# Low-order parts of k in one zero-padded tile per head, so that both score products contract over 128 partitions

## The chip, the cores and the metric

The kernel runs on one core of a Trainium2 chip. Its engines work side by side, each on its own queue in order: TensorE (PE in the profile; PEld are its weight loads), VectorE (DVE), ScalarE (ACT), GpSimd (POOL) and SyncE (SP), which issues most of the DMAs. The metric is the device time of one execution in microseconds, the median of the runs. Times of single instructions come from one profiled execution.

## The reference

A decoder trunk of two layers over 512 tokens of width 1024, in float32. Each layer is half a feed-forward step, a mixer, and half a feed-forward step; a norm stands before each and at the end. The mixer has 12 heads of dilated window attention (three groups of four, with rotary positions on q and k) and 4 heads of stick-breaking attention, 64 features a head:

```
s = einsum('bhrnqd,bhrnkd->bhrnqk', qb, kw) * (dh ** -0.5)      # dilated: banded, causal, softmax
z = einsum('bhqd,bhkd->bhqk', q_blk, k) * (dh ** -0.5)          # stick-breaking
w = where(past, exp(log_sigmoid(z) + after), 0.0)               # after: sum of log_sigmoid(-z) between s and t
y = gate_dil * (o_dil @ w_proj_dil) + gate_sb * (o_sb @ w_proj_sb)
x = x + y @ w_out
```

## The kernel before

Activations lie feature-major, 128 features by 512 tokens in a tile. A float32 product is made of float32r passes: each operand is split into a high part and a low part (value minus high), and high x high, high x low and low x high are added in PSUM. For the large projections that is `mm3` (L141, its three matmuls on L142, L143, L144), fed by the class `Weights`, which streams 128x128 weight blocks from memory and splits them four at a time on ACT (L76) and DVE (L77).

Attention scores have only 64 features a head, and the kernel uses the other 64 partitions for the split. `qk_pair` (L348) projects q and then k of two heads (e = 0, 1) into one PSUM bank, 24 matmuls each. For q it makes a tile per head whose own half of the partitions holds the high part (ACT, L372) and whose other half holds the low part (DVE, L373). For k it makes a tile per head with the high part in its own half (L376) and, by a DMA between partitions, a copy of it in the other half (L377). One tile `kl` for both heads takes the low parts, head 0 in the lower half and head 1 in the upper (L378). With rotary positions ("rope"), DVE multiplies by the cosine table (L357) and shuffles partitions into `qb` (L358), and POOL multiplies and adds (L359, L360).

`scores` (L382) then makes one block of scores from two matmuls into the same PSUM columns: q tile x k high tile over 128 partitions (L384: high x high plus low x high), and q high x k low over the 64 partitions of the head (L385, the slices `own`). The stationary operand is the 128 columns of q in both, loaded for each matmul.

`stick` (L410) runs two heads, each with four query blocks against 128, 256, 384 and 512 keys: scores, a mask as one more matmul (L419), Abs, Exp and Ln on ACT, a scan and two more passes on DVE (L426 to L429), Exp on ACT (L430); then transposes (L439), a split of the transposed weights (`split_t`), and their products with the values (L443). `dil_scores` (L465) makes the scores of three dilated groups for a pair of head slots, 128 or 256 keys at a time, each block masked and reduced on DVE (L481, L497); `dil_softmax` and `dil_values` follow (transposes L556, L558, L573; products with values L565, L583). `gather_o` (L397) collects an output in the tile `of`. `fill` puts gate projections between these.

The mixer's main order in the program is V projection, q and k of heads 0 and 1, stick, q and k of heads 2 and 3, stick, then for two slot pairs scores, softmax and values, then gates and the output projection. The order in which each engine gets its instructions is set before the run by a planner with modelled times (`schedule_with_timeline_sim=True`), so projections of later heads stand between the attention blocks of earlier ones. Tiles are taken from pools with a fixed number of buffers: 10 for q and k tiles (five of them a pair), 2 for `qb`, 1 for `of`. A buffer is given again when its last reader is done.

Of the kernel before, what the change touches and what calls it, by code (L numbers as in the profile page):

```python
# [9 lines left out]
F32 = mybir.dt.float32  # L10
F32R = mybir.dt.float32r
# [4 lines left out]
P = 128  # L16
D = 1024
T = 512
# [12 lines left out]
TAIL = 2  # L31
HELD = KD
HT = T // 2
# Output tiles whose gates are projected after q and k of (slot pair, group);
# group 3 stands for the end of the slot pair.
GATES = {(0, 0): (), (0, 1): (0, 1), (0, 2): (), (0, 3): (2,), (1, 0): (3,), (1, 1): (), (1, 2): (), (1, 3): (4, 5, 6)}

# Activations are feature-major: [feature, token]. Token columns are ordered
# c = 128 j + 32 r + m for the token t = 128 j + 4 m + r ("nat" order); the
# dilated groups use (r, j, m) order ("perm": one 128-token tile per residue r  # L40
# modulo 4). Float32 products run as three float32r passes: hi*hi, hi*lo, lo*hi
# with lo = v - float32r(v).


class Weights:
    """Streams 128x128 weight blocks in order of use, split into hi and lo."""

    AHEAD = 2

# [56 lines left out]
def trunk(ctx, tc, xin, win, gains, rope, masks, out, depth):  # L106
    nc = tc.nc

    def pool(stack, name, bufs=1, **kw):
        return stack.enter_context(tc.tile_pool(name=name, bufs=bufs, reuse_waits="tile", **kw))  # L110
# [6 lines left out]
    npool = pool(ctx, "npool")  # L117
# [11 lines left out]
    for k in range(KD):  # L129
        t = xpool.tile([P, T], F32, name=f"x{k}", tag=f"x{k}")  # L130
# [24 lines left out]
            return nc.scalar.preload_act_table_set(name)  # L155

    class Norm:
        """Gathers the squares of x tile by tile; r = rsqrt(mean + eps)."""

        def __init__(self, g, table=None):  # L160
            self.g = g * KD
# [92 lines left out]
                finale(st, hs, nxt)  # L254

    def finale(st, hs, nxt):
        """The last output tiles by halves of the tokens, each followed by its final norm."""
        op = pool(st, "fin", 4)
        blocks = [[weights.block() for _ in hs] for _ in range(TAIL)]
        for c0 in range(0, T, HT):  # L260
            c = slice(c0, c0 + HT)
            for i, row in enumerate(blocks):
                d = KD - TAIL + i
                ps = bank("o")
                for f, (w, h) in enumerate(zip(row, hs)):
                    mm3(ps[:, :HT], w, [t[:, c] for t in h], f == 0, f == NF - 1)
                nc.vector.scalar_tensor_tensor(xs[d][:, c], ps[:, :HT], 0.5, xs[d][:, c], ALU.mult, ALU.add)
                nxt.square(d, c)
            nxt.finish(c0 // P, (c0 + HT) // P)
            for k in range(0, KD, 2):  # L270
                o = op.tile([P, 2, HT], F32, name="o", tag="o")
                eng = nc.gpsimd if k == 2 else nc.vector
                for i in range(2):
                    eng.tensor_mul(o[:, i], xs[k + i][:, c], nxt.rb[:, :HT])
                nc.sync.dma_start(out[k:k + 2, :, c].rearrange("k p t -> p k t"), o)

    def mixer(norm, nxt):
        outer = ExitStack()
        mp = pool(outer, "mix")
        st = ExitStack()  # L280
        vp = pool(st, "mixv")
        qp = pool(st, "mixq", 10)
        wk = pool(st, "mixw", 2)
        pp = pool(st, "mixp", 8)
        tp = pool(st, "mixt", 2)
# [1 line left out]
        h = norm.h  # L287

        def work(name):
            return wk.tile([P, T], F32, name=name, tag=name, bufs=1 if name == "of" else 2)  # L290

        spill = []
        for k in range(KD):
            t = dram.tile([P, T], F32, name="spill", tag="spill")
# [5 lines left out]
        nc.scalar.dma_start(cr, rope[0])  # L300
        nc.scalar.dma_start(sr, rope[1])

        # V, token-major: [token, head, hi|lo, 64]
        pv = []
        for half in range(2):
            pv.append([bank(b) for b in ("mmtt", "ssoo")[half]])
            for k in range(KD):
                wh, wl = weights.quarter()
                for j in range(NT):
                    c = slice(j * P, (j + 1) * P)  # L310
                    ps = pv[half][j]
# [15 lines left out]
            if half == 0:  # L327
                v0, vs = [], []
                for j in range(NT):
                    sc = norm.rt[:, j:j + 1]  # L330
                    for lst, nm, off in ((v0, "v0", 0), (vs, "vs", 256)):
                        t = vp.tile([P, 4, 2, HD], F32R, name=f"{nm}_{j}", tag=f"{nm}_{j}")
# [13 lines left out]
            return nat_view(ap)  # L346

        def qk_pair(kind, view_q, view_k):  # L348
            """Projects q and k of two heads; returns per head (q stack, k hi, k lo)."""
            res = []  # L350
            for which in ("q", "k"):
                ps = bank("m")
                project(ps, h)
                a = work("qa")
                if kind == "rope":
                    b = work("qb")
                    nc.vector.tensor_mul(a, ps, cr)  # L357
                    nc.vector.stream_shuffle(b, ps, ROT)  # L358
                    nc.gpsimd.tensor_mul(b, b, sr)  # L359
                    nc.gpsimd.tensor_add(a, a, b)  # L360
                else:
                    nc.vector.scalar_tensor_tensor(a, ps, SC if which == "q" else 1.0, norm.rb,
                                                   ALU.mult, ALU.mult)
                if which == "k":
                    kl = qp.tile([P, T], F32R, name="kl", tag="q")
                for e in range(2):
                    own = slice(64 * e, 64 * e + 64)
                    oth = slice(64 - 64 * e, 128 - 64 * e)
                    src = nat_view(a[own])
                    hi = qp.tile([P, T], F32R, name=which + "h", tag="q")  # L370
                    if which == "q":
                        nc.scalar.copy(view_q(hi[own]), src)  # L372
                        nc.vector.tensor_sub(view_q(hi[oth]), src, view_q(hi[own]).bitcast(F32))  # L373
                        res.append([hi])
                    else:
                        nc.scalar.copy(view_k(hi[own]), src)  # L376
                        nc.sync.dma_start(hi[oth].bitcast(F32), hi[own].bitcast(F32))  # L377
                        nc.vector.tensor_sub(view_k(kl[own]), src, view_k(hi[own]).bitcast(F32))  # L378
                        res[e] += [hi, kl, own]
            return res  # L380

        def scores(ps, qkv, qc, kc, start, stop=True):  # L382
            q, kh, kl, own = qkv
            nc.tensor.matmul(ps, q[:, qc], kh[:, kc], start=start, stop=False, skip_group_check=True)  # L384
            nc.tensor.matmul(ps, q[own, qc], kl[own, kc], start=False, stop=stop, skip_group_check=True)  # L385

        def tile_c(i, n=1):
            return slice(i * P, (i + n) * P)
# [6 lines left out]
            return hi, lo  # L395

        def gather_o(po, of, e):  # L397
            """Adds the Vh and Vl halves into of's half e."""
            own = slice(64 * e, 64 * e + 64)
            nc.scalar.copy(of[own], po[64:128])  # L400
            nc.vector.tensor_add(of[own], po[0:64], of[own])
# [57 lines left out]
        gates = {}  # L459
# [3 lines left out]
                gates[d] = (gate(d, 0), gate(d, 1))  # L463

        def dil_scores(s, st_a, st_b, pn, pm):  # L465
            """Scores, mask and running maximum of slots 2s, 2s+1."""
            qk0 = qk_pair("rope", same, same)
            fill(s, 0)
            for e in range(2):
                for i in range(2):  # L470
                    ps = bank("s")
                    for u in range(2):
                        j = 2 * i + u
                        c0 = 256 * u + (0 if j else P)
                        c1 = 256 * u + 256
                        scores(ps[:, c0:c1], qk0[e], tile_c(j), slice(max(j - 1, 0) * P, (j + 1) * P), u == 0)
                    for u in range(2):
                        j = 2 * i + u
                        lo_c = 0 if j else P
                        t = pn[e][j]  # L480
                        nc.vector.tensor_tensor_reduce(  # L481
                            t[:, lo_c:256], ps[:, 256 * u + lo_c:256 * u + 256], mnat[:, lo_c:256],
                            1.0, NEG, ALU.add, ALU.max, st_a[:, 0, e, j:j + 1])
            qk1 = qk_pair("rope", nat_to_perm, nat_to_perm)
            fill(s, 1)
            qk2 = qk_pair("rope", nat_to_perm, nat_to_perm)
            fill(s, 2)
            for e in range(2):
                for i in range(2):
                    ps = bank("s")  # L490
                    for u in range(2):
                        r = 2 * i + u
                        scores(ps[:, 256 * u:256 * u + P], qk1[e], tile_c(r), tile_c(r), u == 0)
                        scores(ps[:, 256 * u + P:256 * u + 256], qk2[e], tile_c(r), tile_c(r), False)
                    for u in range(2):
                        r = 2 * i + u
                        nc.vector.tensor_tensor_reduce(  # L497
                            pm[e][r], ps[:, 256 * u:256 * u + 256], mperm,
                            1.0, NEG, ALU.add, ALU.max, st_b[:, 0, e, r:r + 1])
# [111 lines left out]
        st = ExitStack()  # L611
# [64 lines left out]
ROT = list(range(8, 16)) + list(range(0, 8)) + list(range(16, 32))  # L676


# [1 line left out]
def _tokens():  # L680
    import numpy as np
    c = np.arange(T)
# [35 lines left out]


def _pack_layer(a, l):  # L720
    """Weight blocks [n, 128, 128] of one layer in the order of use."""
    import numpy as np

    def ffn(g, u, dn):
# [78 lines left out]
```

## Time and profile before

| | |
|---|---|
| median of 3 runs | 2210.35 us (2209.13 to 2211.56) |
| profiled execution, first to last instruction | 2208.9 us |
| DVE busy | 1192.9 us (54%) |
| ACT busy | 893.0 us (40%) |
| POOL busy | 366.1 us (17%) |
| mean granted TensorE clock | 0.992 |

A line of the engine views names the line of the kernel, the engine, the output tile and its inputs, the shape and how often it stands; "64*128 64x256" is a product that contracts over 64 partitions, has 128 output rows and streams 256 columns. The mixers lie at about 380 to 700 us and 1475 to 1790 us of the span. The granted clock is the share of full speed at which TensorE was let run.

### The profile page before, as it was taken

How to read it: one execution, taken by the hardware profiler on the slowest of the kernel's cores; microseconds unless marked ns; L12 is line 12 of the kernel's file. 1: busy time of each engine (PE TensorE's matmuls, PEld its weight loads, DVE VectorE, ACT ScalarE, POOL GpSimd, SP SyncE). 2: the span in 40 equal slices, each digit the busy share in tenths (PEclk: the TensorE clock that was granted, in tenths of full speed). 3: DMA queues.
4: the chain of work that ended last, by engine and by line, in shares of the span. 5: the costliest groups of instructions: out<-in, count | busy, mean ns of one | idle time of the engine just before them, and what ended most of it. 6: DMA issues, size and time to landing. Idle time of an engine off the chain costs nothing.

```text
span 2208.9 us, 25967 instructions
## 1 busy us (share of the span) xinstructions
PE 2187.1 (99%) x9828; PEld 1787.4 (81%) x9828; DVE 1192.9 (54%) x1892; ACT 893.0 (40%) x1572; POOL 366.1 (17%) x384
## 2 busy tenths in 40 slices
PE   8999999999999999999999999999999999999998
PEld 7888888877887888888888888888778788888887
DVE  5445433688757545543345544337887575544433
ACT  5333333566454433333233333236654454333332
POOL 2222100021312122210022220000123112222100
PEclk9999999999999999999999999999999999999999
DMA  4233333222213232232222333333222143333322
GB/s 150 95 96 96 100 114 120 88 90 77 77 62 124 96 96 96 96 96 95 96 96 96 96 96 105 109 119 96 81 70 79 58 134 96 96 96 98 99 91 86
DMA packets 64622, 212.81 MB, mean 96 GB/s; under 512 B 7408, under 2 KB 9456, under 8 KB 64496
## 3 DMA queue, kind: packets, MB, share of 16 engines
q1 hardware_dynamic: 63920, 210.10, 29.6%
q8 instruction: 77, 1.26, 0.2%
q10 hardware_dynamic: 576, 1.05, 0.2%
q14 instruction: 49, 0.40, 0.1%
HBM read 200.63 MB, written 6.29 MB: 94 GB/s over the span
## 4 chain that ended last, share of the span: by engine, by line
PE 98%; DVE 1%; ACT 0%; DMA 0%; POOL 0%; issue 0%; SPq 0%; DVEq 0%; POOLq 0%; ACTq 0%
PE ps_o L144 13%; PE ps_o L143 13%; PE ps_o L142 13%; PE ps_m L142 11%; PE ps_m L143 11%; PE ps_m L144 11%; PE ps_t L142 5%; PE ps_t L143 5%; PE ps_t L144 5%; PE ps_s L385 2%; PE ps_s L384 1%; PE ps_o L583 1%; PE ps_o L443 0%; PE ps_t L314 0%; PE ps_m L314 0%; PE ps_m L313 0%
## 5 line engine op out<-in xcount | busy, mean ns | idle before, releaser
L77 DVE TENSOR_TENSOR wlo<-wraw,whi 128x512 fp32r<-128x512 f32 x736 | 595.8, 812 | 617.5 <-ACT whi L76 616.6
L76 ACT CAST whi<-wraw 128x512 fp32r<-128x512 f32 x736 | 456.0, 621 | 1004.7 <-PE ps_o L143 489.4
L142 PE MATMUL ps_m<-xh,whi 128*128 128x512 f32 x992 | 395.3, 399 | 8.9 <-ACT whi L76 5.8
L143 PE MATMUL ps_m<-xl,whi 128*128 128x512 f32 x992 | 394.4, 398 | 0.0
L144 PE MATMUL ps_m<-xh,wlo 128*128 128x512 f32 x992 | 394.2, 397 | 0.0
L142 PE MATMUL ps_o<-fh,whi 128*128 128x512 f32 (+1 forms) x748 | 285.6, 382 | 0.0
L143 PE MATMUL ps_o<-fl,whi 128*128 128x512 f32 (+1 forms) x748 | 285.5, 382 | 0.0
L144 PE MATMUL ps_o<-fh,wlo 128*128 128x512 f32 (+1 forms) x748 | 285.5, 382 | 0.0
L239 POOL TENSOR_TENSOR fg<-fg,fs 128x512 f32<-128x512 f32 x88 | 114.9, 1307 | 928.7 <-ACT fs L238 928.7
L142 PEld LDWEIGHTS ps_m<-xh,whi 128*128 128x128 f32 x992 | 189.6, 191 | 51.1 <-ACT whi L76 6.7
L143 PEld LDWEIGHTS ps_m<-xl,whi 128*128 128x128 f32 x992 | 189.6, 191 | 40.0 <-DVE xl L180 0.8
L144 PEld LDWEIGHTS ps_m<-xh,wlo 128*128 128x128 f32 x992 | 189.8, 191 | 39.5 <-DVE wlo L77 0.2
L142 PE MATMUL ps_t<-xh,whi 128*128 128x512 f32 x480 | 187.0, 390 | 0.0
L143 PE MATMUL ps_t<-xl,whi 128*128 128x512 f32 x480 | 186.8, 389 | 0.0
L144 PE MATMUL ps_t<-xh,wlo 128*128 128x512 f32 x480 | 186.8, 389 | 0.0
L143 PE MATMUL ps_o<-xl,whi 128*128 128x512 f32 x448 | 174.3, 389 | 0.0
L142 PE MATMUL ps_o<-xh,whi 128*128 128x512 f32 x448 | 174.3, 389 | 0.0
L144 PE MATMUL ps_o<-xh,wlo 128*128 128x512 f32 x448 | 174.3, 389 | 0.0
L143 PEld LDWEIGHTS ps_o<-fl,whi 128*128 128x128 f32 x748 | 140.5, 188 | 30.2
L144 PEld LDWEIGHTS ps_o<-fh,wlo 128*128 128x128 f32 x748 | 140.4, 188 | 30.1
L142 PEld LDWEIGHTS ps_o<-fh,whi 128*128 128x128 f32 x748 | 140.5, 188 | 30.0
L240 POOL TENSOR_TENSOR fg<-fg,rb 128x512 f32<-128x512 f32 x88 | 114.9, 1307 | 6.3
(204 smaller groups left out, 2702.3 us busy)
## 6 DMA issues: line engine op xcount, KB each, us to landing
wraw<-in_w_dram SPq DMA_DIRECT2D x367, 512.0 KB, 3.4
spill<-x SPq DMA_DIRECT2D x16, 256.0 KB, 2.1
kh<-kh SPq DMA_DIRECT2D x32, 128.0 KB, 2.8
x<-spill SPq DMA_DIRECT2D x16, 256.0 KB, 3.4
x<-in_x_dram SPq DMA_DIRECT2D x8, 256.0 KB, 5.8
out_dram<-o SPq DMA_DIRECT2D x8, 256.0 KB, 3.0
wraw<-in_w_dram SPq DMA_DIRECT2D x2, 256.0 KB, 4.2
cr<-in_rope_dram ACTq DMA_DIRECT2D x2, 256.0 KB, 2.6
```

The costliest lines, as they stand in the source:

```text
L76: nc.scalar.copy(hi, src)
L77: nc.vector.tensor_sub(lo, src, hi.bitcast(F32))
L142: nc.tensor.matmul(ps, w[0], v[0], start=start, stop=False, skip_group_check=True)
L143: nc.tensor.matmul(ps, w[0], v[1], start=False, stop=False, skip_group_check=True)
L144: nc.tensor.matmul(ps, w[1], v[0], start=False, stop=stop, skip_group_check=True)
L239: nc.gpsimd.tensor_mul(g, g, s)
L240: nc.gpsimd.tensor_mul(g, g, norm.rb)
L384: nc.tensor.matmul(ps, q[:, qc], kh[:, kc], start=start, stop=False, skip_group_check=True)
L385: nc.tensor.matmul(ps, q[own, qc], kl[own, kc], start=False, stop=stop, skip_group_check=True)
L583: nc.tensor.matmul(dst, v, pr[:, c:c + P].rearrange("p (j m) -> p j m", m=32), start=False, stop=False, skip_group_check=True)
```

## The change

Each head gets a tile of its own for the low part of k. The half of the partitions that belongs to the other head is zero, so the product of q and k low may run over all 128 partitions: the low part of q meets zeros. There are two sets of two such tiles, used by turns, and their zeros are written by POOL once in each mixer. The q and k pool goes from 10 to 8 buffers, `qb` from two buffers to one, and `of` takes the buffer `sq` of the norm's squares. Comments were also dropped; they are left out here.

```diff
-        qp = pool(st, "mixq", 10)
+        qp = pool(st, "mixq", 8)
+        zp = pool(st, "mixz")
...
         def work(name):
-            return wk.tile([P, T], F32, name=name, tag=name, bufs=1 if name == "of" else 2)
+            if name == "of":
+                return npool.tile([P, T], F32, name=name, tag="sq")
+            return wk.tile([P, T], F32, name=name, tag=name, bufs=1 if name == "qb" else 2)
+        klo = []
+        for i in range(2):
+            row = []
+            for e in range(2):
+                t = zp.tile([P, T], F32R, name="kl", tag=f"kl{i}{e}")
+                nc.gpsimd.memset(t[64 - 64 * e:128 - 64 * e].bitcast(F32), 0.0)
+                row.append(t)
+            klo.append(row)
+        pairs = [0]
...
                 if which == "k":
-                    kl = qp.tile([P, T], F32R, name="kl", tag="q")
+                    kls = klo[pairs[0] % 2]
+                    pairs[0] += 1
...
-                        nc.vector.tensor_sub(view_k(kl[own]), src, view_k(hi[own]).bitcast(F32))
-                        res[e] += [hi, kl, own]
+                        nc.vector.tensor_sub(view_k(kls[e][own]), src, view_k(hi[own]).bitcast(F32))
+                        res[e] += [hi, kls[e]]
...
         def scores(ps, qkv, qc, kc, start, stop=True):
-            q, kh, kl, own = qkv
+            q, kh, kl = qkv
             nc.tensor.matmul(ps, q[:, qc], kh[:, kc], start=start, stop=False, skip_group_check=True)
-            nc.tensor.matmul(ps, q[own, qc], kl[own, kc], start=False, stop=stop, skip_group_check=True)
+            nc.tensor.matmul(ps, q[:, qc], kl[:, kc], start=False, stop=stop, skip_group_check=True)
```

## The prediction

> **What bounds the kernel now.** I read the page first: the span, the busy line and the chain that ended last.
>
> ```profile
> span 2208.9 us, 25967 instructions
> PE 2187.1 (99%) x9828; PEld 1787.4 (81%) x9828; DVE 1192.9 (54%) x1892; ACT 893.0 (40%) x1572; POOL 366.1 (17%) x384
> ...
> PE 98%; DVE 1%; ACT 0%; DMA 0%; POOL 0%; issue 0%; SPq 0%; DVEq 0%; POOLq 0%; ACTq 0%
> ```
>
> TensorE (PE) carries 98% of the chain, so a microsecond saved on it is a microsecond of the run, wherever VectorE (DVE) is not just as late. But 99% busy doesn't mean 99% used: the records of matmuls overlap, so what a matmul costs is the distance from its start to the next start. That I read from the timeline, in three places of the first mixer. First a burst of the 128-wide score products, high part (L384) and low part (L385) by turns:
>
> ```profile
> 553.22 0.33 PE L384 MATMUL ps_s<-kh,qh 128*128 128x128 f32 x1
> 553.47 0.32 PE L385 MATMUL ps_s<-kl,qh 64*128 64x128 f32 x1
> 553.73 0.33 PE L384 MATMUL ps_s<-kh,qh 128*128 128x128 f32 x1
> ```
>
> One step is 0.25 us and a pair 0.51 us; the engine waits for nobody in it. Then products of the same width that all use 128 rows, the dilated values (L583):
>
> ```profile
> 598.51 0.22 PE L583 MATMUL ps_o<-ptl,v 128*128 128x128 f32 x1
> 598.57 0.28 PE L583 MATMUL ps_o<-pth,v 128*128 128x128 f32 x1
> 598.68 0.28 PE L583 MATMUL ps_o<-ptl,v 128*128 128x128 f32 x1
> ```
>
> Here a step is 0.11 us (the first of the row 0.06), a pair 0.22 us, although each loads a 128x128 stationary block too, and two in a row add into the same PSUM columns with the same stationary block, as the score pairs do. The one difference that remains is the "64*128": the low product uses half of the rows. The trace names no cause, but both steps are long, the one into a 64-row product and the one out of it.
>
> **The change, part by part.** Score products: the low product gets 128 rows, so every matmul of the kernel has them. Counts and widths come from the groups by shape:
>
> ```profile
> L385 PE MATMUL ps_s<-kl,qh 64*128 64x128 f32 x80 | 26.6, 333 | 0.0
> ...
> L385 PE MATMUL ps_s<-kl,qh 64*128 64x256 f32 x32 | 12.2, 381 | 0.0
> ...
> L385 PE MATMUL ps_s<-kl,qh 64*128 64x512 f32 x8 | 4.0, 495 | 0.0
> L385 PE MATMUL ps_s<-kl,qh 64*128 64x384 f32 x8 | 3.5, 437 | 0.0
> ```
>
> Steps of the wider pairs, and of full-row products as wide (L565 for 256, L443 for 512):
>
> ```profile
> 538.35 0.38 PE L384 MATMUL ps_s<-kh,qh 128*128 128x256 f32 x1
> 538.66 0.39 PE L385 MATMUL ps_s<-kl,qh 64*128 64x256 f32 x1
> 538.98 0.39 PE L384 MATMUL ps_s<-kh,qh 128*128 128x256 f32 x1
> ...
> 502.34 0.39 PE L384 MATMUL ps_s<-kh,qh 128*128 128x512 f32 x1
> 502.66 0.50 PE L385 MATMUL ps_s<-kl,qh 64*128 64x512 f32 x1
> 503.09 0.33 PE L419 MATMUL ps_s<-msbr,identr 128*128 128x128 f32 x1
> ...
> 588.26 0.28 PE L565 MATMUL ps_o<-pth,v 128*128 128x256 f32 x1
> 588.38 0.28 PE L565 MATMUL ps_o<-ptl,v 128*128 128x256 f32 x1
> ...
> 521.99 0.39 PE L443 MATMUL ps_o<-pth,vs 128*128 128x512 f32 x1
> 522.22 0.39 PE L443 MATMUL ps_o<-ptl,vs 128*128 128x512 f32 x1
> ```
>
> A 256-wide pair goes from 0.63 to 0.24, taken as 0.38 saved; a 512-wide one from 0.75 to 0.46, 0.29 saved; a 128-wide one from 0.51 to 0.22, 0.29 saved; for 384 I take 0.33, between its neighbours. The sum is 80 x 0.29 + 32 x 0.38 + 8 x 0.33 + 8 x 0.29 = 23.2 + 12.2 + 2.6 + 2.3 = **40.3 us**, or 0.315 a pair over 128 pairs. Steps at the two ends of a burst, next to other matmuls, are counted like those within it; that is left to the range.
>
> How much of it reaches the end depends on the stage, so next I count pairs and other engines by stretch: low products alone (three stretches of the first mixer, with 9, 16 and 39 of its 64), then all engines. The second mixer runs the same program, and I double the counts. The columns are busy time and count of PE, weight loads (and DVE, ACT, POOL), the granted clock, the DMA share and GB/s.
>
> ```profile
> 440.00:481.00 41.00, 3.60 (x9) 1.65 (x9) 1.00 0.32 99
> 481.00:545.00 64.00, 6.21 (x16) 2.93 (x16) 1.00 0.27 79
> 545.00:635.00 90.00, 13.27 (x39) 7.33 (x39) 0.92 0.23 68
> ```
>
> ```profile
> 481.00:545.00 64.00, 63.27 (x284) 49.71 (x285) 55.27 (x99) 39.60 (x76) 11.51 (x8) 1.00 0.27 79
> 545.00:635.00 90.00, 90.00 (x400) 71.92 (x399) 60.91 (x148) 40.90 (x108) 24.03 (x47) 0.92 0.23 68
> ...
> 1637.00:1727.00 90.00, 90.00 (x400) 71.90 (x401) 61.34 (x148) 40.41 (x107) 24.12 (x45) 0.93 0.22 68
> ```
>
> The chain within 451 to 482, in order of time, tells about the first stretch:
>
> ```profile
> 461.84 1.10 DVE wlo L77
> 462.93 2.25 DVE sc L427
> 465.20 0.70 DVE sc L429
> 465.93 1.19 ACT sw L430
> ```
>
> There the scan of the stick-breaking blocks on DVE is the chain, and a faster PE only waits longer: 18 pairs (both mixers), 5.7 us, are worth **0**. In the second stretch DVE is busy 55.27 of 64 us: 32 pairs, 10.1 us, and I take half, **5.1**, since DVE becomes late before all of it is used. In the third DVE is busy 60.91 of 90: 78 pairs, 24.6 us, taken whole, **24.6**.
>
> The clock is the second term. The same stretch shows a granted clock of 0.92 and 0.93, so PE loses 0.08 x 90 + 0.07 x 90 = 13.5 us in the two mixers. It falls right behind a score burst, though PE is busy throughout:
>
> ```profile
> 556.62 0.63 PE L143 MATMUL ps_m<-xl,whi 128*128 128x512 f32 x1
> 557.04 0.63 PE L144 MATMUL ps_m<-xh,wlo 128*128 128x512 f32 x1
> ```
>
> A 512-wide step is 0.42 there instead of 0.23. Where the last values run in bursts of 0.11 steps and no score burst is near, it is 1.00:
>
> ```profile
> 640.00:660.00 20.00, 20.00 (x113) 17.26 (x112) 15.45 (x39) 15.08 (x27) 3.18 (x16) 1.00 0.24 80
> ```
>
> So I read the low rate of products in the 0.25 steps as what lowers it. With 0.11 steps it may stay up; the bounds are 0 and 13.5, and I take two thirds, **9.0**. The Trainium skill ("TensorE: Matmul & The Clock Gate", Part 1) says that the clock falls after about 3.4 us in which the array was idle; PE has no such gap here, so by that rule the falls have another cause, would stay, and the sum would be smaller by 9.0; the trace (0.92 with 90.00 us of 90 busy) does not show the idle window that it asks for.
>
> Other edits. Four POOL memsets of 64x512 in each mixer are not in the trace: from below nothing, from above four times the 1.29 us of a 128x512 product of two inputs, 5.2 us. I take 0, since POOL stands idle for 140 us before it scales the rope tables at 391.23, and no score product stands before 440 us:
>
> ```profile
> 391.23 1.29 POOL L318 TENSOR_TENSOR cr<-cr,rb 128x512 f32<-128x512 f32 x1 [140.45 <-ACT rb L218]
> ...
> 597.56 1.62 POOL L360 TENSOR_TENSOR qa<-qa,qb 128x512 f32<-128x512 f32 x1
> ...
> 601.18 0.73 DVE L358 STREAM_SHUFFLE qb<-ps_m 128x512 f32<-128x512 f32 x1
> ```
>
> Were that cover gone, rope would start up to 5.2 us later in each mixer, and PE has projections to do meanwhile. One qb buffer instead of two adds a wait: DVE's shuffle (L358) must wait until POOL's sum (L360) has read the shuffle before it. Behind the shuffle DVE holds the weight splits (L77) that PE needs. The tightest place is shown: POOL ends at 599.18, and the next shuffle starts at 601.18, 2.0 us later, so the wait is nothing; a late POOL costs what it is late, once per projection. The "of" tile in the norm's square buffer costs nothing: squares and attention outputs lie in different stretches of the run. Eight buffers for four tiles a pair hold two pairs, as ten did for five. DVE, ACT and the DMA copies of kh keep their number and shapes.
>
> **Sum** against the profiled execution: 2208.9 - (0 + 5.1 + 24.6 + 9.0) = 2208.9 - 38.7 = 2170.2. The median of the runs, 2210.35, lies 1.45 above that span; with it **2171.7, stated as 2172 us**.
>
> **Rivals.** (1) DVE takes over and the clock still falls. DVE is at 55.27 of 64 in the second stretch, and parts of the third are as dense; against it stands the third's mean of two thirds. Then three quarters of 24.6 come through and nothing else, 18.5: 2192 us. (2) The step doesn't come from the rows but from a stationary load that isn't hidden. A load and a stream in series would be the recorded load, 0.187 (row below), and the shortest distance shown between 128-wide products, 0.06: some 0.24 against 0.25 now, so 0.01 for each of 256 products, 2.6 us, and no change of clock: 2208 us. The L583 rows speak against it: 0.11 steps with equal rows, loads included. The same page of the Trainium skill says (Part 3, The mechanism) that a load runs beside a matmul in flight only when their row groups differ; by that rule the change would take this overlap away and the result would be this rival's; the L583 rows don't agree with it.
>
> ```profile
> L385 PEld LDWEIGHTS ps_s<-kl,qh 64*128 64x128 f32 x128 | 23.9, 187 | 17.8 <-issue 10.6
> ```
>
> (3) Slower: the order on the engines is planned from modelled times, and the new prices and the single qb may move a rope pair's projections, which fill PE while DVE scans, behind the stick-breaking blocks. One pair is 48 matmuls at 0.23 (the L443 step), 11 us of idle PE per mixer, 22 in both; two pairs a mixer are 44, more than the 38.7 gained: 2216 us. From two pairs on it decides; one pair leaves a gain. For it speaks that PE's filler there is thin; against it, that the same depth of buffers is kept.
>
> **How the numbers follow.** About 0.2%, 4.4 us, is what a measurement of this kernel can tell from no change. The forecast has 0.66: from 2156 (all 40.3 and 13.5 come through) to 2183 (the clock term is nil and a tenth more is lost). Rival 1 has 0.22 (2183 to 2201), rival 2 0.07, rival 3 0.05. So faster 0.88, same 0.07, slower 0.05. The range runs from 2156 to 2197: it takes in the forecast and most of rival 1, and leaves out rivals 2 and 3.
>
> **What would show it.** Right, if L385 stands as 128*128 with steps of 0.11 at 128 wide and 0.12 at 256, if the granted clock of the stretch between the stick-breaking blocks and the last values is near 1.00, and if DVE rows take a larger share of the chain in the first two stretches. Wrong, if pairs still take 0.5 us (rival 2), if PE shows idle time before its score products (rivals 1 and 3), if the shuffle waits for POOL, or if the clock falls in other places.

## The result, and the profile after

| | before | after |
|---|---|---|
| median | 2210.4 us | 2174.2 us (2173.7 to 2175.8) |
| ratio, 95% interval | | 0.9837, 0.9823 to 0.9851 |
| profiled execution | 2208.9 us | 2171.8 us |
| mean granted clock | 0.992 | 0.998 |

The kernel became 36.2 us faster; 2172 had been forecast. The page of the changed kernel, span, busy line and chain:

```profile
span 2171.8 us, 25973 instructions
PE 2140.2 (99%) x9828; PEld 1766.4 (81%) x9828; DVE 1190.5 (55%) x1892; ACT 890.4 (41%) x1572; POOL 369.4 (17%) x392
...
PE 92%; DVE 4%; issue 1%; ACT 1%; POOL 1%; DMA 0%; SPq 0%; DVEq 0%; POOLq 0%; ACTq 0%
```

The number of matmuls is the same; PE's share of the chain fell from 98% to 92%, and DVE, ACT and POOL have pieces of it now. Lines have moved down by some 15: L384 and L385 are now L400 and L401, the shuffle is L373, the dilated values are L599. In the timeline, steps of a score burst in the first mixer:

```profile
600.75 0.27 PE L401 MATMUL ps_s<-kl,qh 128*128 128x128 f32 x1
600.86 0.28 PE L400 MATMUL ps_s<-kh,qh 128*128 128x128 f32 x1
600.98 0.28 PE L401 MATMUL ps_s<-kl,qh 128*128 128x128 f32 x1
601.09 0.28 PE L400 MATMUL ps_s<-kh,qh 128*128 128x128 f32 x1
```

A step is 0.11 us where it was 0.25, and the pair 0.23 where it was 0.51. The clock, by stretches of the two mixers (columns as before: busy time and count of PE, weight loads, DVE, ACT, POOL, granted clock, DMA share, GB/s):

```profile
545.00:635.00 90.00, 88.13 (x465) 73.56 (x464) 68.47 (x173) 53.35 (x130) 28.69 (x74) 1.00 0.27 79
1620.00:1710.00 90.00, 88.16 (x465) 73.62 (x464) 68.58 (x173) 53.50 (x130) 28.67 (x74) 1.00 0.27 80
```

Before, it was 0.92 and 0.93 there. To see which stage gave the time, I take the same four POOL instructions of each mixer as marks: the first rope product, the fourth, the eighth, and the first copy of the second softmax. First mixer, before:

```profile
452.46 1.58 POOL L359 TENSOR_TENSOR qb<-qb,sr 128x512 f32<-128x512 f32 x1 [58.24 <-DVE qb L358]
...
484.46 1.30 POOL L359 TENSOR_TENSOR qb<-qb,sr 128x512 f32<-128x512 f32 x1 [14.24 <-DVE qb L358]
...
551.36 1.27 POOL L359 TENSOR_TENSOR qb<-qb,sr 128x512 f32<-128x512 f32 x1 [5.17 <-DVE qb L358]
...
634.21 4.05 POOL L517 COPY bn<-stb 32x4 f32<-32x4 f32 x16 [28.73 <-ACT pt L512]
```

and after:

```profile
452.37 1.58 POOL L374 TENSOR_TENSOR qb<-qb,sr 128x512 f32<-128x512 f32 x1 [58.88 <-DVE qb L373]
...
484.38 1.30 POOL L374 TENSOR_TENSOR qb<-qb,sr 128x512 f32<-128x512 f32 x1 [14.24 <-DVE qb L373]
...
545.90 1.28 POOL L374 TENSOR_TENSOR qb<-qb,sr 128x512 f32<-128x512 f32 x1 [3.88 <-DVE qb L373]
...
615.08 4.07 POOL L533 COPY bn<-stb 32x4 f32<-32x4 f32 x16 [17.30 <-ACT pt L528]
```

| stage, first mixer | before | after | gained |
|---|---|---|---|
| first to second mark | 32.00 | 32.01 | 0.0 |
| second to third | 66.90 | 61.52 | 5.4 |
| third to fourth | 82.85 | 69.18 | 13.7 |

The same marks of the second mixer stand at 1544.90, 1576.89, 1643.80 and 1726.63 before, and at 1525.94, 1557.94, 1620.89 and 1690.06 after: gains of 0.0, 4.0 and 13.7. Together 36.7 of the 37.1 us between the two spans.

### The profile page after: what moved, and what is told of

Same layout as the page of the kernel before. It is cut to its first block, busy times and chain, and to the rows that moved or that the text cites. A ratio compares the mean times of both kernels' runs of the same rounds, so it can differ in the third digit from the quotient of the medians.

```text
span 2171.8 us, 25973 instructions
## 1 busy us (share of the span) xinstructions
PE 2140.2 (99%) x9828; PEld 1766.4 (81%) x9828; DVE 1190.5 (55%) x1892; ACT 890.4 (41%) x1572; POOL 369.4 (17%) x392
## 4 chain that ended last, share of the span: by engine, by line
PE 92%; DVE 4%; issue 1%; ACT 1%; POOL 1%; DMA 0%; SPq 0%; DVEq 0%; POOLq 0%; ACTq 0%
PE ps_o L142 14%; PE ps_o L143 14%; PE ps_o L144 14%; PE ps_m L142 9%; PE ps_m L143 9%; PE ps_m L144 9%; PE ps_t L142 5%; PE ps_t L143 5%; PE ps_t L144 5%; DVE wlo L77 1%; DVE sc L443 1%; PE ps_o L599 0%; PE ps_s L401 0%; PE ps_s L400 0%; DVE pt L560 0%
## 5 line engine op out<-in xcount | busy, mean ns | idle before, releaser
L142 PE MATMUL ps_m<-xh,whi 128*128 128x512 f32 x992 | 390.7, 394 | 9.9 <-ACT whi L76 6.4
```

What stands on the lines that cost most here:

```text
L142: nc.tensor.matmul(ps, w[0], v[0], start=start, stop=False, skip_group_check=True)
```

## Experiments

Theory: a matmul over 64 rows between matmuls over 128 rows makes both steps long, by some 0.145 us each, and the slow bursts that come of it pull the clock down. Rivals: the new pools and the order planned from them give the gain; a 64-row product is slow by itself; DVE, not PE, sets what the steps are worth. Each kernel below is the changed one with one edit, and the times are medians.

### The low product back on 64 rows, all else as changed

```diff
-                        res[e] += [hi, kls[e]]
+                        res[e] += [hi, kls[e], own]
...
-            q, kh, kl = qkv
+            q, kh, kl, own = qkv
...
-            nc.tensor.matmul(ps, q[:, qc], kl[:, kc], start=False, stop=stop, skip_group_check=True)
+            nc.tensor.matmul(ps, q[own, qc], kl[own, kc], start=False, stop=stop, skip_group_check=True)
```

> The changed kernel with the low product back on the 64 rows of its head; its tiles, pools, memsets and the single qb stay as changed. Theory (the gain comes from the steps between 64-row and 128-row products and from the clock behind them): back at 2210 us, within 5 us, with 0.25 us steps and six falls of the clock as before. Rival (the new pools and the order that the planner makes from them carry part of the gain): below 2200 us. Rival (those edits cost something that the rows pay back): above 2216 us.

2211.8 us; ratio to the kernel before 1.0008 (0.9998 to 1.0017), mean clock 0.992, and 0.92 again in the third stretch of both mixers. The whole gain hangs on the rows of the low product. Memsets, tiles by turns, the single `qb`, the moved `of` and the order planned from them cost or bring nothing that can be told apart.

### 64 rows in the dilated scores alone

With the same tuple as above, and in `scores`:

```diff
-            nc.tensor.matmul(ps, q[:, qc], kl[:, kc], start=False, stop=stop, skip_group_check=True)
+            rows = own if stop else slice(0, P)
+            nc.tensor.matmul(ps, q[rows, qc], kl[rows, kc], start=False, stop=stop, skip_group_check=True)
```

(the dilated part calls with `stop` true, stick-breaking with false).

> The changed kernel with 64-row low products in the dilated scores alone (96 of 128 pairs); stick-breaking scores keep 128 rows. Theory: the third stretch of each mixer (from the last rope projections of the first slot pair to the second softmax) and the clock there are lost again, 12 to 14 us a mixer, so 2198 to 2206 us, with all or nearly all falls of the clock back. Rival (stick-breaking carries as much as dilated): below 2192 us.

2209.6 us, ratio 0.9989 (0.9979 to 0.9999). More was lost than expected: nearly everything. The third stretch of both mixers in this kernel:

```profile
545.00:635.00 90.00, 90.00 (x395) 71.52 (x394) 59.70 (x147) 40.30 (x105) 23.07 (x44) 0.91 0.23 68
1635.00:1725.00 90.00, 90.00 (x394) 71.34 (x393) 60.76 (x147) 39.24 (x100) 24.31 (x44) 0.91 0.23 68
```

The clock is at 0.91 there, lower than in the kernel before, and 0.990 over the run against 0.992. 0.002 of 2209 is 4.4 us, about what stick-breaking with full rows brings by itself (next run). The marks of this kernel bear it out in part: its second stage took 65.79 and 64.28 us (66.90 and 66.91 before), its third 83.77 and 83.82 (82.85 and 82.83 before). So the expectation missed the clock, which fell for longer than in the kernel before; the ten runs of this kernel go from 2201.1 us, with a mean clock of 0.994, to 2212.3, with 0.988.

### 64 rows in the stick-breaking scores alone

The condition turned round: `rows = slice(0, P) if stop else own`.

> The changed kernel with 64-row low products in the stick-breaking scores alone (32 of 128 pairs, 13 us of steps by the counts); dilated scores keep 128 rows. Theory: its first stretch is set by the scan on VectorE and gives nothing back, the second loses half of its steps: 2176 to 2183 us, no fall of the clock in the dilated bursts. Rival (TensorE sets the pace in both stretches): 13 us slower than the changed kernel, 2187 us.

2178.0 us, ratio 0.9855 (0.984 to 0.987): some 4 us slower than the changed kernel, inside what the theory gave. The 13 us of the rival are 10.3 by the prediction's own prices (8 pairs of each width at 0.29, 0.38, 0.33 and 0.29); 4 is well below either. By the marks the first stage took 31.98 and 32.00 us, as in the changed kernel, the second 63.68 and 65.31 (61.52 and 62.95 there), the third 69.20 in both. The clock in the third stretches was 0.98 and 1.00: one fall did come, which the theory had not expected, behind a place where PE had waited (2.34 of 3.40 us busy).

### Both products on 64 rows

```diff
-            nc.tensor.matmul(ps, q[:, qc], kh[:, kc], start=start, stop=False, skip_group_check=True)
-            nc.tensor.matmul(ps, q[:, qc], kl[:, kc], start=False, stop=stop, skip_group_check=True)
+            nc.tensor.matmul(ps, q[own, qc], kh[own, kc], start=start, stop=False, skip_group_check=True)
+            nc.tensor.matmul(ps, q[own, qc], kl[own, kc], start=False, stop=stop, skip_group_check=True)
```

> The changed kernel with both products of a pair on the 64 rows of the head, so the low part of q never meets the high part of k: that pass of the scores is left out. Theory (it is the turn from 64 to 128 rows and back that costs): within a burst there is no turn, steps of 0.11 us at 128 wide, and only the two ends of a burst pay; 2174 to 2186 us. Rival (a 64-row product costs 0.25 us by itself): all 256 products are long, 2205 us or more.

2183.1 us, ratio 0.9877 (0.9862 to 0.9892). The timeline of this kernel at a burst of the first mixer:

```profile
603.35 0.22 PE L599 MATMUL ps_o<-pth,v 128*128 128x128 f32 x1
603.50 0.33 PE L400 MATMUL ps_s<-kh,qh 64*128 64x128 f32 x1
603.66 0.27 PE L401 MATMUL ps_s<-kl,qh 64*128 64x128 f32 x1
603.77 0.28 PE L400 MATMUL ps_s<-kh,qh 64*128 64x128 f32 x1
603.89 0.27 PE L401 MATMUL ps_s<-kl,qh 64*128 64x128 f32 x1
...
604.44 0.27 PE L400 MATMUL ps_s<-kh,qh 64*128 64x128 f32 x1
604.65 0.33 PE L599 MATMUL ps_o<-ptl,v 128*128 128x128 f32 x1
604.81 0.28 PE L599 MATMUL ps_o<-pth,v 128*128 128x128 f32 x1
...
606.26 0.27 PE L599 MATMUL ps_o<-ptl,v 128*128 128x128 f32 x1
606.47 0.33 PE L401 MATMUL ps_s<-kl,qh 64*128 64x128 f32 x1
606.63 0.27 PE L400 MATMUL ps_s<-kh,qh 64*128 64x128 f32 x1
```

Within the 64-row burst a step is 0.11 us, as with 128 rows. Long are the first (0.15 and 0.16, going in), the last (0.21 out of it, then 0.16), and again the first of the next burst (0.21 and 0.16). A 64-row product is not slow; the turn is what costs. The clock did fall in this kernel, behind such a burst (two stretches just before and after):

```profile
600.50:607.30 6.80, 6.80 (x46) 5.99 (x44) 6.46 (x20) 4.32 (x12) 0.00 (x0) 1.00 0.28 48
607.30:614.10 6.80, 6.80 (x21) 5.15 (x21) 4.08 (x12) 4.28 (x15) 0.00 (x0) 0.50 0.17 67
```

### Fewer turns: high and low products of the dilated scores in groups

64-row low products, but per PSUM bank first all high products, then all low ones:

```diff
+        def grouped(blocks, start=True):
+            for ps, (q, kh, kl, own), qc, kc in blocks:
+                nc.tensor.matmul(ps, q[:, qc], kh[:, kc], start=start, stop=False, skip_group_check=True)
+                start = False
+            for ps, (q, kh, kl, own), qc, kc in blocks:
+                nc.tensor.matmul(ps, q[own, qc], kl[own, kc], start=False, stop=True, skip_group_check=True)
...
-                        scores(ps[:, c0:c1], qk0[e], tile_c(j), slice(max(j - 1, 0) * P, (j + 1) * P), u == 0)
+                        blocks.append((ps[:, c0:c1], qk0[e], tile_c(j), slice(max(j - 1, 0) * P, (j + 1) * P)))
+                    grouped(blocks)
```

(and likewise for the other two groups).

> 64-row low products in the dilated scores, as in the run that lost 35 us by them, but per PSUM bank all high products first and then all low ones: two turns of the row count a bank instead of four or eight, 64 in place of 192. Theory (each turn costs some 0.145 us, the difference between steps of 0.255 and 0.11): 128 turns fewer are 18 us, and the falls of the clock become fewer, since the rate in a burst rises; 2183 to 2195 us. Rival (time goes by the number of 64-row products, which is the same): 2207 us or more.

2177.4 us, ratio 0.985 (0.9835 to 0.9864), better than expected: of the 35 us that 64 rows cost pair by pair, 32 come back without padding in the dilated scores (the stick-breaking ones keep it). The timeline merges equal instructions; four low products, four high ones and four low ones again:

```profile
547.46 0.66 PE L408 MATMUL ps_s<-kl,qh 64*128 64x128 f32 x4
548.05 0.66 PE L405 MATMUL ps_s<-kh,qh 128*128 128x128 f32 x4
548.64 0.66 PE L408 MATMUL ps_s<-kl,qh 64*128 64x128 f32 x4
```

Four take 0.59 from start to start, that is three steps of 0.11 and one, the turn, of some 0.25. The clock in the two third stretches was 1.00 throughout. The 18 us that the expectation had for 128 turns fewer leave 14 of the 32, about what a clock of 0.91 costs over two stretches of 90 us (16); that the clock comes back whole was not expected.

### Is DVE what is late now?

Every second low part of the weights goes to POOL in a part of the mixer (`share` is set and cleared in the mixer's body):

```diff
-            nc.vector.tensor_sub(lo, src, hi.bitcast(F32))
+            eng = nc.gpsimd if self.share and self.done % 2 else nc.vector
+            eng.tensor_sub(lo, src, hi.bitcast(F32))
```

First for the stick-breaking projections alone:

> The changed kernel with every second low part of the weights (a 128x512 subtraction) on GpSimd instead of VectorE, from the first stick-breaking projections to the first dilated scores. Theory (VectorE sets the pace there now, and TensorE waits some 4 us a mixer for it): 2167 to 2173 us, TensorE's waits for the scan and the gate in that stretch smaller. Rival (the waits are set by the order or by latency, not by how busy VectorE is): same as the changed kernel, 2172 to 2177 us. Rival (GpSimd, with 1.3 to 1.6 us for one, delivers the weights late): 2178 us or more.

2175.0 us, ratio 0.9836 (0.982 to 0.9853): no change. On POOL no split stands between 441 and 545 us, since the projections that run beside the stick-breaking blocks are those of the dilated part, whose weights were not shared. Even so the first stage took 27.9 and 27.8 us in the two mixers, in place of 32.0; the third took 81.2 in place of 69.2, with some 50 more products in it. So the planner had made another order, and the total stayed. The low parts of k on POOL besides:

> The kernel with shared weight splits, and the low parts of k (64x512 subtractions, two a pair) on GpSimd too. Theory as there: 2165 to 2172 us. Rival (k's low part then comes later than TensorE wants its low product): slower than the kernel with shared weight splits alone.

2176.2 us, 0.9843 (0.9829 to 0.9858), no gain either. The changed kernel beside these:

> The changed kernel once more, beside the three others on the same chip: 2172 to 2177 us.

2173.3 us, 0.983 (0.9815 to 0.9845). Then the splits shared over the whole attention part, and until the end of the first slot pair:

> Every second low part of the weights on GpSimd from the first stick-breaking projections to the end of the second slot pair (in the first such kernel only the splits for the stick-breaking projections were shared, since those of the rotary projections, which run beside the stick-breaking blocks, are asked for by the dilated part). Theory (VectorE sets the pace of the attention part wherever TensorE waits): those waits shrink over the whole part, 2164 to 2171 us. Rival (the order that the planner makes, and GpSimd's own queue with its copies for the softmax, give it back): 2172 to 2178 us.

> The same, but shared only until the end of the first slot pair. Theory: 2165 to 2172 us. Rival as there: 2172 to 2178 us.

2166.1 us, ratio 0.9795 (0.9778 to 0.9813), and 2170.5 us, 0.9817 (0.98 to 0.9835). The first is faster than the changed kernel by some 7 us (the intervals of the ratios don't overlap) and the fastest of all. The stretch of the stick-breaking scan in the changed kernel and in this one, after and then shared:

```profile
451.00:484.00 33.00, 28.38 (x136) 22.73 (x135) 28.09 (x45) 20.51 (x43) 9.32 (x6) 1.00 0.26 72
```

```profile
451.00:484.00 33.00, 32.03 (x154) 26.59 (x153) 28.67 (x43) 19.66 (x40) 17.42 (x12) 1.00 0.30 88
```

PE gets 154 matmuls done in place of 136 while DVE is as busy as before, and POOL's busy time nearly doubles. The first stage took 27.3 us in both of these kernels. That would fit DVE as what PE waited for, but the first kernel of these had 27.9 there with no split on POOL in it. What parts the three is the third stage: 69.7 us where the splits were shared over the whole part, 75.3 where they were shared for the first slot pair, 81.2 where they stopped before it (first mixer each). Whether the 7 us come from work taken off DVE or from the order planned anew is not shown.

## Why the prediction came out

**The bound and the cause of the long steps** were right. PE's step, not its busy share, was the thing to read, and the two 64-row runs confirm the "one difference that remains": the turn, in both directions. Its size, 0.255 less 0.11, was right as well. Of the signs that were named, the steps, the clock of the third stretch and DVE's larger share of the chain in the first came; in the second stretch DVE's share did not grow. Two signs against it came too, both small: PE waits before score products (for the scan's result, 3.9 us in all), and the clock falls in a new place.

**The first stretch, 0 of its 5.7 us**: right to the digit, 32.00 us before and 32.01 after. The chain of waits of the changed kernel goes through DVE there as it did before:

```profile
461.76 1.10 DVE wlo L77
462.86 2.24 DVE sc L443
465.12 0.70 DVE sc L445
465.84 1.13 ACT sw L446
```

and PE waits in the open now (its timeline; the scan's result is what ends it):

```profile
464.25 0.39 PE L142 MATMUL ps_m<-xh,whi 128*128 128x512 f32 x1
465.96 0.36 PE L400 MATMUL ps_s<-kh,qh 128*128 128x256 f32 x1 [1.32 <-DVE sc L445]
```

**The second stretch, half of 10.1 us**: too little. Between the marks it gave 9.3 us. The marks hold 19 pairs a mixer in place of 16; by their widths they are worth 6.3 each. In the first mixer PE also did more between the marks than before (316 products in place of 304), so the pairs came through whole. In the second it came in late, behind a fall of the clock (below), and had 321 to do; in the other profile of the changed kernel, which has no fall there, the stage took 61.6 us in both mixers. The chain of the stage (484 to 546 us) stays with PE:

```profile
by line: PE ps_m L142 26.7%; PE ps_m L144 26.4%; PE ps_m L143 26.3%; PE ps_o L459 6.1%; PE ps_s L401 4.9%; PE ps_s L400 4.6%; PE ps_t L455 4.5%; PE ps_s L435 0.7%
```

So the step that took half for DVE failed: DVE, at 86% before and busy 57.06 of 62 us after, was not yet a bound.

**The third stretch, all of 24.6 us, and the clock, 9.0 of 13.5**: the clock was under-sized and the pairs over-sized. The granted clock went from 0.92 and 0.93 to 1.00, so nearly all of the 13.5 came; one new fall stands in the first stretch of the second mixer, behind a place where PE waits:

```profile
1525.00:1558.00 33.00, 28.65 (x133) 22.83 (x132) 28.09 (x46) 20.51 (x44) 9.36 (x7) 0.95 0.27 74
```

0.05 x 33 is 1.7 us. The time of that stage did not grow by it (32.00 us), but the next stage took 62.95 us in place of the 61.52 of the first mixer. That the clock would stay up was right in the main; the reason given, the rate of the products, was not (last section). Between the marks the third stage gave 27.3 us. The clock's part of it is 0.08 x 83 = 6.6 in the first mixer and about as much in the second, 13 in all; 14 remain for the pairs. The marks hold 36 pairs a mixer, worth some 11 each, so about 8 of 22 us were lost. The chains of that stage show its shares by line, before and after, and then two pieces of the one after:

```profile
by line: PE ps_m L144 22.7%; PE ps_m L142 22.4%; PE ps_m L143 22.2%; PE ps_s L385 11.6%; PE ps_s L384 10.3%; PE ps_o L583 4.4%; PE ps_t L573 2.2%; PE ps_o L565 2.2%; PE ps_t L556 1.1%; PE ps_t L558 0.8%; PE ps_o L443 0.4%
```

```profile
by line: issue 18.2%; PE ps_m L143 9.5%; PE ps_m L142 9.3%; PE ps_m L144 9.0%; DVE wlo L77 6.4%; DVE pt L560 6.1%; POOL bn L533 5.0%; DVE ptl L410 4.1%; DVE qh L389 3.4%; PE ps_o L599 3.0%; PE ps_s L401 3.0%; DVE pt L557 2.9%; DVE qa L372 2
...
577.35 1.68 DVE qh L389
...
579.06 1.84 DVE wlo L77 x2
```

Before, the chain of the stage was PE alone; after, DVE has many pieces of it, and 18% is time with no cause shown. PE's waits in the open there are short: 67.45 of 69 us busy, with 1.3 us of waits for DVE by name (0.7 for `ptl`). The rest of the 8 us lies in steps drawn out under records that overlap, and which engine drew out each was not shown. So "taken whole" failed, most likely for the reason that rival 1 had, dense places of DVE: its mean load was 79% (54.76 of 69 us), below that of the second stage, where nothing was lost. The sum came within 2 us because the errors cancel, which is luck: second stretch 4 too little, clock 4 too little, third stretch 10 too much; some 2 of the last are pairs that the marks count to the second stage.

**The edits costed at nothing** were nothing: the first experiment measures them together at 1.0008. POOL wrote the four zero halves within 2.24 us at 373.93 and then stood idle for 14 us before it scaled the tables, so the bound of 5.2 us was wide enough.

**Rival 2**, a load that isn't hidden, and with it the rule of the Trainium skill ("TensorE: Matmul & The Clock Gate", Part 3) as the prediction took it, is refuted for this kernel: with equal rows throughout, steps are 0.11 us with a load of 0.19 us in each. **Rival 3** did not come: the stage from which it would have taken projections took the same time.

## What to carry to other kernels

Between matmuls over all 128 partitions, a matmul over 64 makes two steps slow, more than double at 128 columns: look at start-to-start steps, next to a run of products of the same width, before believing in a busy TensorE. Either pad with zeros so that the row count stays, or group the products so that it turns seldom; the two are worth nearly the same here. And the mean load of the next engine doesn't tell what of a stage's saving comes through: here all of it came at 92%, and about two thirds at 79%. Look at the chain of the stage instead. Work moved off that engine paid here only when it was moved over the whole attention part, and a new order that the planner makes may be as much of the cause.

## What the runs showed of the hardware that was not expected

The clock doesn't need an idle TensorE to fall, as far as busy time tells (the ends of matmul records are modelled). Before, it was granted at 0.92 and 0.93 over stretches with 90.00 of 90 us busy. The stretch just before a fall to 0.50, first in the kernel before (fall at 556.5 us), then in the changed one (1554.8), then in the changed one run again (1660.9):

```profile
553.10:556.50 3.40, 3.40 (x14) 2.54 (x15) 2.60 (x9) 1.90 (x4) 0.88 (x1) 1.00 0.08 13
```

```profile
1551.40:1554.80 3.40, 1.54 (x13) 1.19 (x11) 2.50 (x6) 2.24 (x4) 0.00 (x0) 1.00 0.00 0
```

```profile
1657.50:1660.90 3.40, 2.35 (x16) 1.83 (x15) 3.37 (x9) 0.62 (x1) 0.92 (x1) 1.00 0.44 115
```

Nor is it the rate of instructions, as the prediction read it: with both products on 64 rows the steps were 0.11 us, as in the changed kernel, and the clock fell to 0.50 behind that burst with PE busy throughout. With 128 rows, or with groups of 128 and 64 rows by turns, no fall in the mixers stands behind a burst in which PE did not wait; those of the changed kernel came behind waits. The work done in the array, columns times rows per time, puts the bursts in order: in columns of 128 rows per us, 376 by turns (192 rows in 0.51 us a pair) and 582 with 64 rows (0.11 us), both with falls, then 651 in groups (four of each in 1.18 us) and 1164 with 128 rows (0.11 us). That this is what is measured on the chip was not shown. The Trainium skill ("TensorE: Matmul & The Clock Gate", Part 1) speaks of idle windows; the traces don't agree for the falls before the change, with 3.40 of 3.40 us busy, and show stretches only partly idle before those after it.

A turn of the row count costs some 0.145 us, in the slow bursts of the kernel before as where it comes singly, in both directions: there it is spread over two steps (0.21 and 0.16, going in or out, against 0.11 each, are 0.15 more).
